# Modulation vectors of a diffusion layer: raw weight tiles of 64 rows by two column halves

## The chip, the cores and the metric

The kernel runs on one core of a Trainium2 chip. The metric is the device time of one execution in microseconds (us). The kernel before was run three times: 2631.08 us in the median, 2630.84 to 2632.65. A core has five engines, each with its own in-order list of instructions: TensorE (PE in the profile; its weight loads are listed apart as PEld), VectorE (DVE), ScalarE (ACT), GpSimd (POOL) and SyncE (SP). SP computes nothing; it issues nearly all transfers. The transfers themselves are moved by 16 DMA engines, which all queues share.

## The reference

One layer over 1024 latent tokens and 256 context tokens of width 1024, all in float32. A first FFN (width 2816), then a mixer (a short gated convolution and grouped-query attention, merged), then a second FFN. Each is normalised and modulated by vectors that come from two conditioning vectors, one for the latent and one for the context tokens. The change concerns only how these vectors are computed:

```python
mod_lat = (silu(c)     @ w_mod + b_mod)      # w_mod: 1024 x 9216
mod_ctx = (silu(c_ctx) @ w_mod + b_mod)
ml, mc = split(mod_lat, 9), split(mod_ctx, 9)   # nine vectors of 1024 each
# first FFN: shift ml[0], scale ml[1], gate ml[2]; mixer: 3, 4, 5; second FFN: 6, 7, 8
# context tokens use mc[0] to mc[4] here
```

So `w_mod` (37.7 MB) is read once, for one or two rows on the left: a matrix-vector product per conditioning vector (a "stream").

## The kernel before

All matrix products are split into a high and a low part (float32r) and made of three matmuls each, with 512 moving columns. The FFNs and the mixer's input products use a seven-product scheme (`Winograd`), whose left operands are weight tiles of 128 columns, fetched to one of three `raw` buffers, split by ScalarE (high part) and VectorE (low part) or first summed by GpSimd.

The modulations are numbered 0 to 8, and each is done in two halves of 512 columns. Modulations 0 and 1 for the latent stream are computed at the very start by other functions (`first_mod`, `second_mod`), for both streams only the first half of modulation 1. The rest are "later modulations", and `later_mod` (L272) computes them. For each half it takes eight raw tiles of 128 rows by 512 columns of `w_mod`, 256 KB each (L285). VectorE multiplies each tile, row by row, by a column of `silu_c`, and adds it to an accumulator `macc`, a tile of 128 x 512 for each stream (L289 and L291). The accumulator then has to be summed over its 128 partitions. It is split into two parts (L298), TensorE multiplies both by a single column of ones (L304, L305), ScalarE copies the resulting row of 512 out of PSUM in an order that suits the next step (L307), one transfer turns the row into four columns (L311), and VectorE adds the bias (L313).

`later_mod` is a generator. A call of `run(steps, n)` in the main loops advances it by n steps, and so its work lies between the products of the main computation. One half is 19 steps: eight with a load and its multiplications, four of waiting (`WAIT`), six more after the split, one at the end. In the first products, run by column tile j, `STEPS` (L42) gives 7 or 6 steps a tile for j up to 12, 11 from 14 on, and in between two for each of 14 context products. Modulation 1 (second half, context only), modulation 0 (context only), the context's first normalisation and modulations 2 to 4 (both streams) come in that order (`all_later_mods`, L1160). Modulation 5 is advanced 8 steps at a time from the mixer's input products (L1361), 6 and 7 8 steps at a time from the attention heads' products (L1442), and 8 by 3 steps a tile in the second FFN (L1828). For 6 and 7 the raw tiles come from a larger pool: four tiles of 512 KB for each half, fetched together (`by_four`, L277 and `fetch_mod`, L316).

Elsewhere the raw tiles and the accumulators come from a pool of eleven tiles of 128 x 512 that they share with the partial results of the main products (`ttile`, L116). The order of the instructions on each engine comes from the framework's scheduler, which plans with its own costs, except where an instruction is pinned (`pinned=True`, `strict`). All recorded operations show line L90, that of a helper, so that the views are read by the names of the tiles.

Of the kernel before, what the change touches and what calls it, by code (L numbers as in the profile page):

```python
# [9 lines left out]
F32 = mybir.dt.float32  # L10
F32R = mybir.dt.float32r
I32 = mybir.dt.int32
AF = mybir.ActivationFunctionType
ALU = mybir.AluOpType
# [4 lines left out]
P = 128  # L19
D = 1024  # L20
KD = D // P
# [22 lines left out]
WAIT = 4  # L44
# [7 lines left out]
def tile_dit_layer(  # L52
# [44 lines left out]
    act, dve, pool, pe, sp = (Engine(e) for e in (nc.scalar, nc.vector, nc.gpsimd, nc.tensor, nc.sync))  # L97

    const = ctx.enter_context(tc.tile_pool(name="const", bufs=1))
# [9 lines left out]
    def uniq(s):  # L109
        n_tiles[0] += 1  # L110
        return f"{s}_{n_tiles[0]}"

    def atile(name, shape=(P, SLOT), dt=F32):
        return apool.tile(list(shape), dt, tag="A", name=uniq(name))

    def ttile(name, n=512, dt=F32):  # L116
        t = tpool.tile([P, 512], dt, tag="t", name=uniq(name))
        return t[:, :n]

    def small(name, n, dt=F32):  # L120
        return spool.tile([P, n], dt, tag=f"s{n}_{name}", name=uniq(name))
# [4 lines left out]
    def ps_t(n=512):  # L126
        return psum.tile([P, 512], F32, tag="t", name=uniq("pt"), bufs=2)[:, :n]
# [4 lines left out]
    def matmul(out, w, x, start, stop, pinned=False, on=False):  # L132

        inst = pe.matmul(out, w, x, start=start, stop=stop, skip_group_check=on)
        if pinned:
            tc.keep_in_program_order(inst)
# [7 lines left out]
    def load(out, in_, pinned=False):  # L144
        inst = sp.dma_start(out=out, in_=in_)
        if pinned:
            tc.keep_in_program_order(inst)
# [6 lines left out]
    ones_r = const.tile([P, 1], F32R, name="ones_r")  # L154
# [4 lines left out]
    bcol = const.tile([P, 72], F32, name="bcol")  # L159
# [26 lines left out]
    def col(name, k=0):  # L186
        o = voff[name] + k
        return cols[:, o : o + 1]

    silu_c = const.tile([P, 16], F32, name="silu_c")  # L190
    act.activation(out=silu_c[:], in_=cols[:, :16], func=AF.Silu)

    modl = const.tile([P, 72], F32, name="modl")
    modc = const.tile([P, 40], F32, name="modc")


    def split(src, hi, lo, lo_eng=None, hi_eng=None):

        if hi_eng is dve:
            dve.tensor_copy(out=hi, in_=src)  # L200
        else:
            act.copy(out=hi, in_=src)
        (lo_eng or dve).tensor_sub(out=lo, in0=src, in1=hi.bitcast(F32))
# [65 lines left out]
            transpose(pr[:, j * P : (j + 1) * P], y[:, j : j + 1].to_broadcast([P, P]), pinned=True)  # L269
        return pr  # L270

    def later_mod(m, halves=(0, 1), streams=None, by_four=False):  # L272

        if streams is None:
            streams = (0, 1) if m < 5 else (0,)
        for half in halves:
            raws = fetch_mod(m, half, False) if by_four else None  # L277
            accs = [ttile(f"macc{v}") for v in streams]
            o = m * D + half * 512
            for k in range(KD):  # L280
                if by_four:
                    raw = raws[k // 2][:, k % 2]
                else:
                    raw = ttile("rawm")
                    load(out=raw, in_=w_mod[0, k * P : (k + 1) * P, o : o + 512])  # L285
                for acc, v in zip(accs, streams):
                    s = silu_c[:, v * 8 + k : v * 8 + k + 1]
                    if k == 0:
                        dve.tensor_scalar(out=acc, in0=raw, scalar1=s, scalar2=None, op0=ALU.mult)  # L289
                    else:  # L290
                        dve.scalar_tensor_tensor(out=acc, in0=raw, scalar=s, in1=acc, op0=ALU.mult, op1=ALU.add)  # L291
                yield
            for _ in range(WAIT):
                yield
            parts = []
            for acc in accs:
                ah, al = ttile("acch", dt=F32R), ttile("accl", dt=F32R)
                split(acc, ah, al)  # L298
                parts.append((ah, al))
            for _ in range(6):  # L300
                yield
            for (ah, al), v in zip(parts, streams):
                mod, pm = (modl, modc)[v], ps_t()
                matmul(pm[:1], ones_r[:], ah, start=True, stop=False, pinned=True)  # L304
                matmul(pm[:1], ones_r[:], al, start=False, stop=True, pinned=True)  # L305
                row = ttile("mrow")
                act.copy(  # L307
                    out=row[:1].rearrange("o (p j) -> o j p", j=4), in_=pm[:1].rearrange("o (j p) -> o j p", j=4)
                )
                mcol = small("mcol", 4)  # L310
                sp.dma_start(out=mcol[:], in_=row[:1])  # L311
                c0 = m * 8 + half * 4
                dve.tensor_add(out=mod[:, c0 : c0 + 4], in0=mcol[:], in1=bcol[:, c0 : c0 + 4])  # L313
            yield

    def fetch_mod(m, half, pinned=True):  # L316
        raws = []
        for kk in range(KD // 2):
            raw = atile("rawm", (P, 2, 512))
            o = m * D + half * 512  # L320
            load(raw[:], w_mod[0, kk * 256 : (kk + 1) * 256, o : o + 512].rearrange("(a p) n -> p a n", p=P), pinned)
            raws.append(raw)
        return raws
# [65 lines left out]
    def part_gain(t, m, gname, s, a, b):  # L389
        mod, c0, o = (modl if s == "l" else modc), (m + 1) * 8, voff[gname]  # L390
        dve.tensor_scalar(
            out=t[:, a:b], in0=mod[:, c0 + a : c0 + b], scalar1=1.0, scalar2=math.sqrt(D), op0=ALU.add, op1=ALU.mult
        )
        dve.tensor_mul(out=t[:, a:b], in0=t[:, a:b], in1=cols[:, o + a : o + b])
# [47 lines left out]
    def modulated_norm(xs, hh, hl, ch, gain, mod, m):  # L442

        s, o, n = ch
        acc = sum_squares(xs, ch)
        for _ in range(3):
            yield
        y = rstd_cols([acc], n, D)
        for _ in range(WAIT if m else WAIT + 3):
            yield  # L450
        pr = bcast(y, n)
        for k in range(KD):
            if k:
                yield
            t = ttile("nt", n)
            dve.tensor_mul(out=t, in0=xs(k, ch), in1=pr)
            dve.tensor_scalar(
                out=t, in0=t, scalar1=gain[s][:, k : k + 1], scalar2=mod[s][:, m * 8 + k : m * 8 + k + 1],
                op0=ALU.mult, op1=ALU.add,
            )  # L460
            split(t, hh(k, ch), hl(k, ch))
        yield
# [638 lines left out]
    for k in range(4):  # L1101
        if k % 2:
            half1.shifted(h0[k][:, 0], k, xh[k])
        else:
            dve.tensor_scalar(
                out=h0[k][:, 0], in0=xh[k], scalar1=gain1["l"][:, k : k + 1], scalar2=modl[:, k : k + 1],
                op0=ALU.mult, op1=ALU.add,
            )
        half1.keep(1, k, h0[k][:, 0])
    start = half1.start_by_half()  # L1110
# [46 lines left out]
    hc = Context("h1ch", F32R), Context("h1cl", F32R)  # L1157
    normc = modulated_norm(xc, *hc, CC, gain1, mods, 0)

    def all_later_mods():  # L1160
        yield from later_mod(1, (1,), (1,))
        yield from later_mod(0, (0, 1), (1,))
        part_gain(gain1["c"], 0, "g1", "c", 0, 8)
        for _ in normc:
            yield
        for m in range(2, 5):
            yield from later_mod(m)

    steps = all_later_mods()
    mix_steps, late_steps, last_steps = later_mod(5), (step for m in (6, 7) for step in later_mod(m, by_four=True)), later_mod(8)  # L1170

# [64 lines left out]
    for j in range(NH):  # L1236
        half1.side = side(j) if j >= SIDE_FROM else None
        u, c = half1.next_first()
        v, b = half1.second(u)
# [115 lines left out]
    for i in range(KD):  # L1355
# [6 lines left out]
        for ch, bg, gc in mixed():  # L1362
            gate(gcd, i, ch, gc)
            o = ch[1]
            y = ttile("y")
            dve.tensor_scalar(out=y, in0=u[:, o : o + 512], scalar1=col("w1", i), scalar2=None, op0=ALU.mult)
            for j in (0, 2):
                a, b = max(o, 1 - j), min(o + 512, L + 1 - j)
                ya = y[:, a - o : b - o]
                dve.scalar_tensor_tensor(  # L1370
                    out=ya, in0=u[:, a + j - 1 : b + j - 1], scalar=col(f"w{j}", i), in1=ya, op0=ALU.mult, op1=ALU.add
# [383 lines left out]
    for ch in (C0, C1):  # L1755
        o = ch[1]
        for d in range(KD):
# [7 lines left out]
                out=xs(d, ch), in0=ps, scalar=modl[:, 40 + d : 41 + d], in1=xs(d, ch), op0=ALU.mult, op1=ALU.add  # L1765
# [12 lines left out]
        out=gf[:], in0=cols[:, voff["gf"] : voff["gf"] + 8], scalar1=math.sqrt(D), scalar2=None, op0=ALU.mult  # L1778
# [47 lines left out]
    for j in range(NH):  # L1826
# [3 lines left out]
        v, b = fast.second(u)  # L1830
# [81 lines left out]
```

## Time and profile before

| | before |
|---|---|
| median of three runs | 2631.08 us |
| span of the profiled execution (the page gives no other time of it) | 2631.1 us |
| TensorE busy | 2609.9 us, 99% |
| VectorE busy | 1997.4 us, 76% |
| ScalarE busy | 1183.5 us, 45% |
| GpSimd busy | 545.8 us, 21% |
| moved by DMA | 384.69 MB, 146 GB/s |

The page lists, for each engine, how long it was busy and how many instructions it ran; then the span in 40 slices; then the DMA queues with packets, megabytes and the share of the sixteen engines' time; then the chain of work that ended last; then groups of equal instructions by `out<-in`, with count, total busy time and mean duration in ns, and behind the bar the idle time before them and what ended it. The waits view lists who waited for whom, in us, times, and the longest. `rawm` is a raw tile of `w_mod`, `macc` an accumulator, `acch` and `accl` its two parts, `mrow` the summed row, `mcol` the columns, `modl` and `modc` the finished vectors of the two streams.

### The profile page before, as it was taken

To read this page: it belongs to the slowest core of one execution; us is meant where nothing else is said; L and a number is where in the kernel's file an instruction comes from. 1 tells how busy PE (TensorE), PEld (TensorE's weight loads), DVE (VectorE), ACT (ScalarE), POOL (GpSimd) and SP (SyncE) were. 2 spreads that over 40 slices of the span, in tenths; PEclk is the share of its full clock that TensorE was granted. 3 is DMA by queue.
4 is the path that set the end of the run, shared out by engine and by line. 5 is a ranking of instruction groups with operands and counts; after the bars stand their busy time and mean duration, and the time that the engine had idled before them with its cause. 6 is when DMAs were issued, how large, how long until landed. Compare 5 with 4: busy or idle time off the path is not lost.

```text
span 2631.1 us, 35379 instructions
## 1 busy us (share of the span) xinstructions
PE 2609.9 (99%) x12665; PEld 2176.1 (83%) x12665; DVE 1997.4 (76%) x3360; ACT 1183.5 (45%) x2343; POOL 545.8 (21%) x425
## 2 busy tenths in 40 slices
PE   8999999999999999999999999999999999999998
PEld 5888899888888888888888888888888888888888
DVE  5888976877897879977788576676457886667996
ACT  6533454333454642333355566574237333334553
POOL 0133201221010034333022112132000442321100
PEclk9999999999999999999999999999999999999999
DMA  8665465345973365542522322113425653227831
GB/s 324 205 210 182 149 215 173 106 131 185 327 184 117 124 205 160 163 134 89 200 77 85 86 87 65 33 37 118 158 85 176 201 167 96 90 80 286 191 84 65
DMA packets 372905, 384.69 MB, mean 146 GB/s; under 512 B 19686, under 2 KB 256376, under 8 KB 372728
## 3 DMA queue, kind: packets, MB, share of 16 engines
q1 hardware_dynamic: 363288, 363.52, 42.1%
q0 software_dynamic: 9440, 18.91, 4.3%
q8 instruction: 99, 1.62, 0.2%
q14 instruction: 78, 0.64, 0.1%
HBM read 310.45 MB, written 71.86 MB: 145 GB/s over the span
## 4 chain that ended last, share of the span: by engine, by line
PE 94%; DVE 3%; DMA 1%; ACT 1%; issue 1%; SPq 0%; DVEq 0%; ACTq 0%
PE ps L90 81%; PE pt L90 8%; PE po L90 6%; DMA rawm<-in_w_mod_dram 1%; DVE xb L90 0%; DVE wl L90 0%; DVE macc L90 0%; DVE m L90 0%; DVE y L90 0%; DVE pts L90 0%; DMA xtok<-in_x_dram 0%; DVE x L90 0%; DVE r L90 0%; SPq L90 0%; DVE rs_t L90 0%
## 5 line engine op out<-in xcount | busy, mean ns | idle before, releaser
L90 PE MATMUL ps<-r,wl 128*128 128x512 f32 x5196 | 1198.3, 390 | 3.6 <-ACT r L90 1.3
L90 PEld LDWEIGHTS ps<-r,wl 128*128 128x128 f32 x5196 | 972.4, 188 | 207.7 <-ACT r L90 1.6
L90 ACT CAST wl<-sum 128x512 fp32r<-128x512 f32 x218 | 134.1, 622 | 294.4 <-PE ps L90 227.1
L90 ACT CAST wl<-raw 128x512 fp32r<-128x512 f32 x287 | 178.2, 622 | 193.1 <-PE ps L90 147.9
L90 DVE TENSOR_TENSOR wl<-raw,wl 128x512 fp32r<-128x512 f32 x287 | 210.2, 736 | 61.0 <-ACT wl L90 59.3
L90 DVE TENSOR_TENSOR wl<-sum,wl 128x512 fp32r<-128x512 f32 x218 | 196.9, 904 | 33.5 <-ACT wl L90 32.3
L90 POOL TENSOR_TENSOR sum<-raw 128x512 f32<-128x512 f32 x55 | 76.4, 1389 | 680.6 <-DMA raw<-in_ffn_w_in_dram 345.3
L90 DVE SCALAR_TENSOR_TENSOR macc<-rawm,silu_c,macc 128x512 f32<-128x512 f32 x178 | 145.4, 835 | 17.1 <-DMA rawm<-in_w_mod_dram 16.6
L90 DVE TENSOR_TENSOR u<-u,ps 128x512 f32<-128x512 f32 x186 | 126.5, 680 | 32.2 <-PE ps L90 32.1
L90 ACT CAST rh<-hid 128x512 fp32r<-128x512 f32 x132 | 82.2, 623 | 139.4 <-PE ps L90 112.3
L90 POOL TENSOR_TENSOR sum<-raw,sum 128x512 f32<-128x512 f32 x55 | 76.7, 1395 | 287.0 <-DVE wl L90 284.0
L90 DVE TENSOR_TENSOR pts<-pt,pts 128x512 fp32r<-128x512 f32 x160 | 107.3, 686 | 36.2 <-ACT pts L90 34.6
L90 DVE TENSOR_REDUCE m<-ps 128x1 f32<-128x256 f32 (+1 forms) x192 | 111.0, 597 | 29.4 <-PE ps L90 28.5
L90 ACT CAST pts<-pt 128x512 fp32r<-128x512 f32 x160 | 92.2, 597 | 85.5 <-PE pt L90 84.4
L90 PE MATMUL ps<-rh,wl 128*128 128x512 f32 x360 | 122.8, 390 | 0.0
L90 PE MATMUL ps<-wh,r 128*128 128x512 f32 x384 | 120.7, 392 | 0.0
L90 DVE TENSOR_TENSOR rl<-hid,rh 128x512 fp32r<-128x512 f32 x132 | 91.0, 693 | 29.9 <-ACT rh L90 19.4
L90 ACT CAST wh<-raw 128x512 fp32r<-128x512 f32 (+1 forms) x85 | 68.2, 803 | 95.5 <-PE ps L90 74.9
L90 PE MATMUL ps<-kl,qs 128*128 128x512 f32 x384 | 104.0, 394 | 0.1
L90 PE MATMUL ps<-rh,wh 128*128 128x512 f32 x300 | 102.8, 389 | 0.0
L90 PE MATMUL ps<-y,wc 128*128 128x512 f32 x384 | 95.3, 391 | 0.2 <-DVE g L90 0.2
L90 POOL TENSOR_TENSOR sum<-sum,raw 128x512 f32<-128x512 f32 x55 | 87.8, 1597 | 5.7 <-PE ps L90 3.9
(325 smaller groups left out, 5102.3 us busy)
## 6 DMA issues: line engine op xcount, KB each, us to landing
raw<-in_ffn_w_in_dram SPq DMA_DIRECT2D x131, 512.0 KB
raw<-in_ffn_w_out_dram SPq DMA_DIRECT2D x72, 512.0 KB
raw<-in_w_in_dram SPq DMA_DIRECT2D x64, 512.0 KB
rawm<-in_w_mod_dram SPq DMA_DIRECT2D x104, 256.0 KB
hid<-hd SPq DMA_DIRECT2D x40, 512.0 KB
ucd<-uc SPq DMA_DIRECT2D x33, 512.0 KB
rawm<-in_w_mod_dram SPq DMA_DIRECT2D x32, 512.0 KB
ws<-in_ffn_w_out_dram POOLq DMA_DIRECT2D x26, 512.0 KB, 6.4
```

The source lines that it names most:

```text
L90: inst = getattr(self.engine, name)(*args, **kw)
```

## The change

`later_mod` now takes a modulation's two halves together, in tiles of 64 rows by all 1024 columns. The left half of the columns goes to partitions 0 to 63 of a raw tile of 128 x 512, the right half to partitions 64 to 127, by one transfer of 256 KB whose source is a view of three dimensions (half, row, column). There are 16 such tiles for a modulation instead of twice eight, so as many transfers and as many multiplications. The column by which a tile is multiplied has to hold the same 64 numbers twice, so `spread_silu` builds `silu_r` from `silu_c` by four small transfers between SBUF tiles, issued before the later modulations begin. The accumulator holds the left half's sums in its upper 64 partitions and the right half's in its lower 64; two one-hot columns (`halves_r`) instead of one of ones sum each half apart, in one pair of matmuls with a result of two rows. Two transfers instead of one turn these rows into columns.

A modulation is now 16 + 4 + 6 + 1 = 27 steps instead of 38. The calls that advance it are unchanged. For modulations 6 and 7 the four larger tiles are each filled by two transfers of 256 KB. The one half that remains alone (modulation 1, second half) keeps the old form as `later_half`.

```diff
+    one_hot = const.tile([P, 2], F32, name="one_hot")
+    pool.memset(one_hot[:], 0.0)
+    for h in range(2):
+        pool.memset(one_hot[h * 64 : (h + 1) * 64, h : h + 1], 1.0)
+    halves_r = const.tile([P, 2], F32R, name="halves_r")
+    act.copy(out=halves_r[:], in_=one_hot[:])
+    silu_r = const.tile([P, 32], F32, name="silu_r")
+
+    def spread_silu():
+        by = silu_r[:].rearrange("p (a s) -> p a s", s=2)
+        for h in range(2):
+            for i in range(2):
+                sp.dma_start(out=by[h * 64 : (h + 1) * 64, :, i], in_=silu_c[i * 64 : (i + 1) * 64, :])
...
-    def later_mod(m, halves=(0, 1), streams=None, by_four=False):
+    def later_mod(m, streams=None, by_four=False):
...
-        for half in halves:
-            raws = fetch_mod(m, half, False) if by_four else None
-            accs = [ttile(f"macc{v}") for v in streams]
-            o = m * D + half * 512
-            for k in range(KD):
-                if by_four:
-                    raw = raws[k // 2][:, k % 2]
+        def rows(t):
+            return w_mod[0, t * 64 : (t + 1) * 64, m * D : (m + 1) * D].rearrange("r (h n) -> h r n", h=2)
+
+        accs = [ttile(f"macc{v}") for v in streams]
+        for t in range(16):
+            if by_four and t % 8 == 0:
+                raws = []
+                for i in range(4):
+                    raw = atile("rawm", (P, 2, 512))
+                    for a in range(2):
+                        load(raw[:, a], rows(t + 2 * i + a))
+                    raws.append(raw)
+            if by_four:
+                raw = raws[t % 8 // 2][:, t % 2]
+            else:
+                raw = ttile("rawm")
+                load(raw, rows(t))
+            for acc, v in zip(accs, streams):
+                s = silu_r[:, v * 16 + t : v * 16 + t + 1]
...
+        yield from mod_sums(accs, streams, m * 8, halves_r, 2)
...
+    def mod_sums(accs, streams, c0, sums, n):
...
+        for (ah, al), v in zip(parts, streams):
+            mod, pm = (modl, modc)[v], ps_t()
+            matmul(pm[:n], sums[:], ah, start=True, stop=False, pinned=True)
+            matmul(pm[:n], sums[:], al, start=False, stop=True, pinned=True)
...
+            mcol = small("mcol", 8)
+            for h in range(n):
+                sp.dma_start(out=mcol[:, h * 4 : (h + 1) * 4], in_=row[h : h + 1])
+            dve.tensor_add(out=mod[:, c0 : c0 + 4 * n], in0=mcol[:, : 4 * n], in1=bcol[:, c0 : c0 + 4 * n])
...
+    spread_silu()
+
     def all_later_mods():
-        yield from later_mod(1, (1,), (1,))
-        yield from later_mod(0, (0, 1), (1,))
+        yield from later_half(1, 1, (1,))
+        yield from later_mod(0, (1,))
```

More of the change, by code (lines that the diff above doesn't have):

```diff
@@ L270, in bcast @@
         return pr
-    def later_mod(m, halves=(0, 1), streams=None, by_four=False):
+    def later_mod(m, streams=None, by_four=False):
         if streams is None:
             streams = (0, 1) if m < 5 else (0,)
-        for half in halves:
-            raws = fetch_mod(m, half, False) if by_four else None
-            accs = [ttile(f"macc{v}") for v in streams]
-            o = m * D + half * 512
-            for k in range(KD):
-                if by_four:
-                    raw = raws[k // 2][:, k % 2]
-                else:
[L284 to L313, printed above, removed]
-            yield
@@ new lines, in rows @@
+        def rows(t):
[16 more added lines that the diff above has]
+                s = silu_r[:, v * 16 + t : v * 16 + t + 1]
+                if t == 0:
+                    dve.tensor_scalar(out=acc, in0=raw, scalar1=s, scalar2=None, op0=ALU.mult)
+                else:
+                    dve.scalar_tensor_tensor(out=acc, in0=raw, scalar=s, in1=acc, op0=ALU.mult, op1=ALU.add)
+            yield
@@ new lines, in later_mod, with later_half @@
+        yield from mod_sums(accs, streams, m * 8, halves_r, 2)
+    def later_half(m, half, streams):
+        accs = [ttile(f"macc{v}") for v in streams]
+        o = m * D + half * 512
+        for k in range(KD):
+            raw = ttile("rawm")
+            load(out=raw, in_=w_mod[0, k * P : (k + 1) * P, o : o + 512])
+            for acc, v in zip(accs, streams):
+                s = silu_c[:, v * 8 + k : v * 8 + k + 1]
+                if k == 0:
+                    dve.tensor_scalar(out=acc, in0=raw, scalar1=s, scalar2=None, op0=ALU.mult)
+                else:
+                    dve.scalar_tensor_tensor(out=acc, in0=raw, scalar=s, in1=acc, op0=ALU.mult, op1=ALU.add)
+            yield
+        yield from mod_sums(accs, streams, m * 8 + half * 4, ones_r, 1)
@@ new lines, in mod_sums @@
+    def mod_sums(accs, streams, c0, sums, n):
+        for _ in range(WAIT):
+            yield
+        parts = []
+        for acc in accs:
+            ah, al = ttile("acch", dt=F32R), ttile("accl", dt=F32R)
+            split(acc, ah, al)
+            parts.append((ah, al))
+        for _ in range(6):
+            yield
+        for (ah, al), v in zip(parts, streams):
+            mod, pm = (modl, modc)[v], ps_t()
+            matmul(pm[:n], sums[:], ah, start=True, stop=False, pinned=True)
+            matmul(pm[:n], sums[:], al, start=False, stop=True, pinned=True)
+            row = ttile("mrow")
+            act.copy(
+                out=row[:n].rearrange("o (p j) -> o j p", j=4), in_=pm[:n].rearrange("o (j p) -> o j p", j=4)
+            )
+            mcol = small("mcol", 8)
+            for h in range(n):
+                sp.dma_start(out=mcol[:, h * 4 : (h + 1) * 4], in_=row[h : h + 1])
+            dve.tensor_add(out=mod[:, c0 : c0 + 4 * n], in0=mcol[:, : 4 * n], in1=bcol[:, c0 : c0 + 4 * n])
+        yield
```

## The prediction

> **What bounds the kernel now.** I read the page first: the span, the engines' busy time, the queue that carries the transfers, the chain that ended last.
>
> ```profile
> span 2631.1 us, 35379 instructions
> PE 2609.9 (99%) x12665; PEld 2176.1 (83%) x12665; DVE 1997.4 (76%) x3360; ACT 1183.5 (45%) x2343; POOL 545.8 (21%) x425
> ...
> q1 hardware_dynamic: 363288, 363.52, 42.1%
> ...
> PE 94%; DVE 3%; DMA 1%; ACT 1%; issue 1%; SPq 0%; DVEq 0%; ACTq 0%
> ```
>
> TensorE is busy 99% of the span and is 94% of the chain. Whatever leaves TensorE shortens the time; whatever leaves VectorE or ScalarE does not; and anything that makes TensorE wait for its weights lengthens the time directly. The sixteen DMA engines are 42.1% busy with the queue that SyncE (SP) feeds: slack on average, as long as all sixteen share it.
>
> Next the waits, SyncE's own queue first, then VectorE's.
>
> ```profile
> SPq L90 <- DVE wl L90: 480.9, 142, 44.7
> ...
> SPq L90 <- DVE macc L90: 18.0, 13, 6.8
> ...
> SPq L90 <- DMA rawm<-in_w_mod_dram: 9.0, 14, 1.8
> ```
>
> ```profile
> DVE macc L90 <- DMA rawm<-in_w_mod_dram: 25.0, 21, 4.0
> ```
>
> SyncE waits longest (480.9 us) until the splitting of a weight tile frees its buffer: weights are fetched as early as a buffer is free, so a stock of fetched weights normally lies ready. The modulation's accumulation waits for its own transfers only 25.0 us in all, so these transfers are prompt today.
>
> **The change, part by part.** The groups that the change touches:
>
> ```profile
> L90 PE MATMUL ps<-r,wl 128*128 128x512 f32 x5196 | 1198.3, 390 | 3.6 <-ACT r L90 1.3 <-DVE r L90 0.8 <-ACT uc L90 0.7
> ...
> L90 DVE SCALAR_TENSOR_TENSOR macc<-rawm,silu_c,macc 128x512 f32<-128x512 f32 x178 | 145.4, 835 | 17.1 <-DMA rawm<-in_w_mod_dram 16.6
> ...
> L90 ACT COPY mrow<-pt 1x512 f32<-1x512 f32 x23 | 24.2, 1079 | 16.9 <-PE pt L90 16.9
> ...
> L90 DVE TENSOR_TENSOR accl<-macc,acch 128x512 fp32r<-128x512 f32 x26 | 17.7, 686 | 2.2 <-ACT acch L90 2.0
> ...
> L90 ACT CAST acch<-macc 128x512 fp32r<-128x512 f32 x26 | 16.2, 622 | 34.2 <-DVE macc L90 32.7 <-DMA hid<-hd 1.5
> ...
> L90 DVE TENSOR_SCALAR macc<-rawm,silu_c 128x512 f32<-128x512 f32 x26 | 12.8, 510 | 8.4 <-DMA rawm<-in_w_mod_dram 8.4
> ...
> L90 PE MATMUL pt<-acch,ones_r 128*1 128x512 f32 x23 | 9.1, 396 | 0.0
> L90 PE MATMUL pt<-accl,ones_r 128*1 128x512 f32 x23 | 9.1, 396 | 0.0
> ```
>
> *Sums over partitions (TensorE).* There are 23 of them, one per half and stream: 1 for the second half of modulation 1, 2 for modulation 0, 12 for 2 to 4, 8 for 5 to 8. After, one serves both halves: 1 + 1 + 6 + 4 = 12. Eleven pairs go, 22 matmuls. One lasts 396 ns, but matmuls overlap: the largest group takes 1198.3 us for 5196, 0.231 us each, and that is what a matmul costs on the path. Gain: 22 x 0.231 = 5.1 us. Two stationary columns instead of one change nothing I can price: the moving 512 columns are the same.
>
> *ScalarE and VectorE.* Eleven casts (622 ns), eleven copies (1079 ns) and eleven subtractions (686 ns) go; the accumulating operations stay 16 per modulation and stream, with eleven first ones (510 ns) turned into later ones (835 ns), +3.6 us of VectorE. Net -18.7 us of ScalarE and -3.9 us of VectorE, at 45% and 76% busy: nothing on the path; TensorE's 99% covers it, and if that cover went, the gain would be at most these amounts.
>
> *Set-up.* The memsets and the copy for the one-hot columns are a handful of instructions in the first microseconds: 0. Four transfers copy 4-byte elements, 1024 each, and sit on SP's queue ahead of the later modulations' loads.
>
> ```profile
> rinvd<-rinv POOLq DMA_DIRECT2D x16, 2.0 KB, 8.6
> ...
> mcol<-mrow SPq DMA_DIRECT2D x23, 2.0 KB
> ```
>
> The nearest row is the 2 KB of 4-byte elements that lands in 8.6 us. Four such in a row, each twice as many elements, are 69 us if nothing overlaps, and nearly 0 if the elements spread over the engines behind the stock of weights. I take 0, since the first user comes 20 steps later; the upper end belongs to the range. The column transfers stay 23 (two for each of 11, one for the half), and their sums cost the same.
>
> *The accumulators* hold one of eleven shared tiles per stream for 20 steps instead of 12. The 18.0 us that SyncE waits for them bound that from above; I take 0.
>
> *The transfers.* This part decides. Until now a raw tile is 128 rows of 2 KB, with 128 as the outermost count on both sides. Now the source is 2 halves of 64 rows: its outermost count is 2, because no single step leads from the 64th row of one half to the first row of the other. How such a transfer is shared among the sixteen engines no row of before shows. If it is cut by its outermost dimension, only two pieces can be made, and two engines carry it; if by rows, sixteen carry it. The price comes from the early stretch in which little but such rows is moved:
>
> ```profile
> DMA packets 1594, 4.02 MB, mean 365 GB/s; under 512 B 118, under 2 KB 140, under 8 KB 1594
> ...
> q1 hardware_dynamic: 1594, 4.02, 97.1%
> ...
> rawm<-in_w_mod_dram SPq DMA_DIRECT2D x8, 512.0 KB
> ```
>
> That window is 3 to 14 us: 0.971 x 16 x 11 = 171 us of engine time for 4.02 MB, 42.5 us per MB. A raw tile of 0.262 MB takes 11.1 us of engine time: 0.70 us on sixteen engines, 5.6 us on two. I take two: the cut needs a dimension that both ends have, and the destination's 128 partitions and the source's 2 x 64 rows agree in nothing outermost but 2. The Trainium skill, "DMA: Bandwidth & Descriptors" (the section on why a DMA increments its semaphore by 16, and its rules for kernel authors), says as much: the engine count is the largest up to 16 that divides both sides' slowest dimension, and an outermost dimension of size c confines the whole transfer to c engines. No run here shows it yet; by it the sum is the one that follows, and by a cut into rows the sum would be only the 5.1 us gained.
>
> Eight modulations (0 and 2 to 8) have 16 such loads each. The weights' loads are queued behind them on the same SP queue, and a sixteenth of every weight tile still passes the two busy engines. On VectorE, the multiplication by a raw tile waits, with the splits of weights and of attention operands queued behind it, and TensorE behind those. A stretch of loads therefore takes what the two engines need: loads x 5.6 us plus their ordinary share. How fast the loads come is set by the steps. The column transfers mark 19 steps per half (8 loads, then 4 + 6 + 1 empty):
>
> ```profile
> 177.85 0.56 SPq L90 DMA_DIRECT2D mcol<-mrow  x1
> 262.30 0.48 SPq L90 DMA_DIRECT2D mcol<-mrow  x1
> 408.27 0.48 SPq L90 DMA_DIRECT2D mcol<-mrow  x1
> 636.75 0.48 SPq L90 DMA_DIRECT2D mcol<-mrow  x1
> 1131.86 0.47 SPq L90 DMA_DIRECT2D mcol<-mrow  x1
> 1227.57 0.48 SPq L90 DMA_DIRECT2D mcol<-mrow  x1
> 1291.01 0.47 SPq L90 DMA_DIRECT2D mcol<-mrow  x1
> 1338.53 0.48 SPq L90 DMA_DIRECT2D mcol<-mrow  x1
> 2148.27 0.48 SPq L90 DMA_DIRECT2D mcol<-mrow  x1
> 2252.11 0.48 SPq L90 DMA_DIRECT2D mcol<-mrow  x1
> ```
>
> First column: the start. Two halves, 38 steps, from 177.9 to 262.3: 2.2 us a step in the first products. Four halves from 408.3 to 636.8: 3.0. One from 1131.9 to 1227.6 (mixer): 5.0. Three from 1291.0 to 1338.5 (heads): 0.83. One from 2148.3 to 2252.1 (second FFN): 5.5. The same stretches by windows; the last two columns are the DMA share and GB/s:
>
> ```profile
> 177.80:262.30 84.50, 84.50 (x374) 69.46 (x373) 74.47 (x102) 28.48 (x49) 34.25 (x24) 1.00 0.63 197
> 262.30:322.00 59.70, 59.70 (x277) 49.83 (x276) 55.94 (x103) 25.42 (x51) 17.41 (x12) 1.00 0.44 141
> ...
> 408.30:636.70 228.40, 228.31 (x1240) 196.49 (x1239) 177.32 (x267) 88.27 (x155) 51.02 (x32) 1.00 0.39 125
> ...
> 1131.90:1227.60 95.70, 95.70 (x424) 79.02 (x423) 71.34 (x111) 31.70 (x53) 30.50 (x20) 1.00 0.35 113
> ...
> 1291.00:1338.50 47.50, 47.50 (x217) 38.63 (x216) 42.00 (x111) 17.92 (x54) 8.34 (x16) 1.00 0.40 133
> ...
> 2148.30:2252.10 103.80, 103.80 (x459) 85.77 (x458) 73.25 (x101) 33.69 (x56) 32.31 (x22) 1.00 0.37 116
> ```
>
> From each share I take off the raw tiles' own part (0.70 us each). A modulation is now 16 loads and 11 empty steps, so the loads come as densely as before but in runs of 16. Excess = loads x 5.6 + share x time - time:
> - modulation 0: 16 loads in 36 us, share 0.50: 90 + 18 - 36 = 72
> - modulation 2: the shorter steps of 0 let it begin 11 steps earlier, among the first products: 11 loads in 24 us, 0.44: 62 + 11 - 24 = 49; its other 5 in 15 us, 0.29: 28 + 4 - 15 = 17
> - modulations 3 and 4: 16 loads in 48 us, 0.29: 90 + 14 - 48 = 56 each
> - modulation 5: 16 in 81 us, 0.29: 90 + 23 - 81 = 32
> - modulations 6 and 7: 32 in 54 steps, 45 us, 0.16: 179 + 7 - 45 = 141 (16 more issues on SP than now, nothing beside that)
> - modulation 8: 16 in 87 us, 0.32: 90 + 28 - 87 = 31
>
> Together 454 us. Against it stands the stock. Two of the three weight buffers lie ready; a pair feeds five products of twelve matmuls, 60 x 0.231 = 13.9 us, and a little is already split: 15 us for each of eight stretches, 120 us. Net +334, less 5.1: 2631.1 + 329 = 2960 us. The span (2631.1) equals the median of the runs (2631.08), so nothing needs adding around it.
>
> Ends: with no stock +454; with the whole queue's price (42.1% x 16 x 2631.1 us / 363.52 MB = 48.8 us per MB, 6.4 us a tile) another 0.8 x 128 = 102; with the set-up's 69 us beyond a stock of 15 another 54: 3236. With a stock of 30 us everywhere (the split tiles too) the eight terms shrink to 227; with the loads also spread into the empty steps, 5 and 8 vanish and 3 and 4 halve, about 130; with the heads' term halved too, because only VectorE and not the weights waits there, about 75: 2701.
>
> **The rivals.**
> *Shared by rows.* Sixteen engines carry the new transfer, 0.70 us each, as now. For it: bytes, row length and destination partitions are the old ones. Against it: the count of 2 in front. Then only the 22 matmuls count: 2631.1 - 5.1 = 2626.0, not slower. It decides if more than about ten engines carry a tile: up to 1.1 us, loads at 2.2 us a step leave room. The Trainium skill, in the same page's rules for kernel authors, advises one 128-partition transfer over two for the halves, since both use the same engines; that speaks for this side if the source's count does not matter, and the sum by it would be these 2626.0.
> *Two engines, but hidden.* On average they have room: 0.421 x 2631.1 + 128 x (5.6 - 0.7) = 1735 us of 2631. If loads came no closer than every 10 us (5.6 over the free share of 0.56), nothing would stall: also 2626.0. Against it: steps of 0.83 to 5.5 us.
> *VectorE becomes the bound*, its operations held in order behind raw tiles: in the sum already, as the heads' 141; if that delay ran in full in every stretch, that is the end without stock, 3080. It has no chance of its own.
>
> **How the numbers follow.** Two engines with stalls 0.85, by rows 0.11, two engines hidden 0.04. The likeliest gives 2960. Between its ends, 2700 to 3230, lies some 0.95 of its chance, 0.81 of the whole, so the range need not reach to the rivals; it is slower throughout. A measurement of this kernel can tell about 0.2%, 5.3 us, from no change. The rivals' -5.1 us sits at that edge: of their 0.15, 0.06 faster, 0.06 within, and 0.03 slower through the set-up transfers or the accumulators. Slower in all 0.88.
>
> **What would show it.** Right: as many bytes moved, VectorE's wait of macc for rawm in hundreds of us instead of 25.0; TensorE's busy share falling below 93% with gaps in the stretches above, the heads' the largest; GB/s in those stretches falling well under the values above; 12 pairs of partition sums. Wrong: rawm waits of tens of us and TensorE still at 99%, which means that sixteen engines shared the tiles; or waits only in the heads, which means that the stock covered the rest.

## The result and the profile after

| | before | after |
|---|---|---|
| median of four runs | 2631.42 us | 3084.92 us (3080.86 to 3087.14) |
| span of the profiled execution | 2631.1 us | 3082.0 us |

The ratio is 1.1718 (95%: 1.1702 to 1.1735): 17% slower, 453.5 us. (Of the six runs of the version with rows outermost, tried below, one took 3732.22 us at a granted clock of 0.653 and is left out of its ratio; its 2640.1 us is the same with or without that run.) The page of the kernel after, its heads, engines, slices of TensorE and its clock, and SP's queue:

```profile
span 3082.0 us, 35318 instructions
PE 2711.3 (88%) x12643; PEld 2232.4 (72%) x12643; DVE 1973.8 (64%) x3338; ACT 1160.7 (38%) x2322; POOL 533.6 (17%) x428
...
PE   8976869586999999869943799999999978999999
...
PEclk9988989797999999989976899999999989999999
...
q1 hardware_dynamic: 365912, 363.53, 36.3%
```

The same 363.5 MB are moved in more time, so the mean share of the DMA engines falls (42.1% to 36.3%) while VectorE waits 442.1 us for raw tiles: the mean over sixteen engines hides what two of them do. TensorE's idle time is span less busy: 21.2 us before, 370.7 us after, so 349.5 of the 450.9 us of longer span. The other 101.4 us are a longer busy time, although 22 matmuls fewer ran: the second row of digits shows the clock below 9 tenths only in slices where TensorE has gaps. (The chain of waits can't be read here: the page follows it over 15% of the span and then loses it.)

The waits and groups of after that answer to those shown of before, VectorE's, SyncE's, TensorE's and the two groups that were priced:

```profile
DVE macc L90 <- DMA rawm<-in_w_mod_dram: 442.1, 120, 7.2
...
PE ps L90 <- DVE wl L90: 162.9, 47, 17.8
```

```profile
SPq L90 <- DVE wl L90: 597.2, 153, 45.8
...
SPq L90 <- DVE macc L90: 34.9, 11, 5.4
```

```profile
L90 PE MATMUL ps<-r,wl 128*128 128x512 f32 x5196 | 1266.7, 403 | 160.6 <-DVE wl L90 112.0
...
L90 DVE SCALAR_TENSOR_TENSOR macc<-rawm,silu_r,macc 128x512 f32<-128x512 f32 x165 | 122.1, 756 | 413.9 <-DMA rawm<-in_w_mod_dram 413.9
```

TensorE's wait for the low part of the weight tiles, 162.9 us, was this before:

```profile
PE ps L90 <- DVE wl L90: 0.7, 2, 0.4
```

VectorE's wait for raw tiles went from 25.0 to 442.1 us, in 120 pieces of at most 7.2 us. That number lies so near the loss that it invites a conclusion; the third experiment shows why it would be the wrong one.

How a raw tile comes is best seen in the heads, where from 1549 to 1662 us nothing else is loaded. First the transfers of that window, then VectorE's timeline:

```profile
GB/s 67 51 51 49 49 50 50 49 58 51 49 49 50 50 49 49 51 49 49 50 50 49 49 51 49 49 50 50 49 49 51 49 46 50 49 50 49 50 50 49
...
q1 hardware_dynamic: 2808, 5.65, 13.2%
```

```profile
1565.54 0.75 DVE L90 SCALAR_TENSOR_TENSOR macc<-rawm,silu_r,macc 128x512 f32<-128x512 f32 x1 [4.51 <-DMA rawm<-in_w_mod_dram]
...
1581.37 0.75 DVE L90 SCALAR_TENSOR_TENSOR macc<-rawm,silu_r,macc 128x512 f32<-128x512 f32 x1 [4.45 <-DMA rawm<-in_w_mod_dram]
1586.64 0.75 DVE L90 SCALAR_TENSOR_TENSOR macc<-rawm,silu_r,macc 128x512 f32<-128x512 f32 x1 [4.45 <-DMA rawm<-in_w_mod_dram]
1591.91 0.75 DVE L90 SCALAR_TENSOR_TENSOR macc<-rawm,silu_r,macc 128x512 f32<-128x512 f32 x1 [4.45 <-DMA rawm<-in_w_mod_dram]
```

13.2% of sixteen engines is 2.1 engines, and 0.132 x 16 x 113 us for 5.65 MB is 42.2 us of engine time per MB, the 42.5 of the prediction. A tile comes every 5.27 us (1581.37, 1586.64, 1591.91). Two engines carry it. The rule of the Trainium skill that the prediction weighed ("DMA: Bandwidth & Descriptors", the section on why a DMA increments its semaphore by 16) agrees with this row.

Where the time went by stretch shows in when the same instructions are issued, first before, then after, in SP's timeline (start, duration): the 13th store `hd<-c` (of the first column tile behind the context products), the first `gcd<-b` of the mixer, the last `yd<-y`, the first `zd<-g` behind the heads, the last `hd<-c` of the second FFN.

```profile
461.14 0.33 SPq L90 DMA_DIRECT2D hd<-c  x1
971.20 0.57 SPq L90 DMA_DIRECT2D gcd<-b  x1
1249.45 0.33 SPq L90 DMA_DIRECT2D yd<-y  x1
1429.91 0.32 SPq L90 DMA_DIRECT2D zd<-g  x1
2399.91 0.37 SPq L90 DMA_DIRECT2D hd<-c  x1
```

```profile
632.61 0.33 SPq L90 DMA_DIRECT2D hd<-c  x1
1197.58 0.57 SPq L90 DMA_DIRECT2D gcd<-b  x1
1528.24 0.33 SPq L90 DMA_DIRECT2D yd<-y  x1
1829.54 0.32 SPq L90 DMA_DIRECT2D zd<-g  x1
2850.68 0.69 SPq L90 DMA_DIRECT2D hd<-c  x1
```

The delay stands at 171.5, 226.4, 278.8, 399.6 and 450.8 us. It grows where raw tiles are loaded; between the heads and the second FFN's first store, where none are, it moves from 399.6 to 400.3.

### The profile page after: what moved, and what is told of

Its sections match the earlier page's. It is cut to its first block, busy times and chain, and to the rows that moved or that the text cites. A ratio compares the mean times of both kernels' runs of the same rounds, so it can differ in the third digit from the quotient of the medians.

```text
span 3082.0 us, 35318 instructions
## 1 busy us (share of the span) xinstructions
PE 2711.3 (88%) x12643; PEld 2232.4 (72%) x12643; DVE 1973.8 (64%) x3338; ACT 1160.7 (38%) x2322; POOL 533.6 (17%) x428
## 3 DMA queue, kind: packets, MB, share of 16 engines
q1 hardware_dynamic: 365912, 363.53, 36.3%
## 5 line engine op out<-in xcount | busy, mean ns | idle before, releaser
L90 PE MATMUL ps<-r,wl 128*128 128x512 f32 x5196 | 1266.7, 403 | 160.6 <-DVE wl L90 112.0
L90 PEld LDWEIGHTS ps<-r,wl 128*128 128x128 f32 x5196 | 1003.8, 195 | 400.6 <-DVE wl L90 133.6
L90 DVE SCALAR_TENSOR_TENSOR macc<-rawm,silu_r,macc 128x512 f32<-128x512 f32 x165 | 122.1, 756 | 413.9 <-DMA rawm<-in_w_mod_dram 413.9
L90 PE MATMUL ps<-h1ch,wl 128*128 128x256 f32 x448 | 95.6, 311 | 37.1 <-DVE wl L90 33.0
L90 ACT ACTIVATE c<-c 128x512 f32<-128x512 f32 x46 | 29.1, 632 | 254.4 <-DMA c<-ucd 163.8
L90 PEld LDWEIGHTS ps<-h1ch,wl 128*128 128x128 f32 x448 | 80.7, 217 | 41.9 <-DVE wl L90 35.1
```

The costliest lines, as they stand in the source:

```text
L90: inst = getattr(self.engine, name)(*args, **kw)
```

## The experiments

The theory was the prediction's: the count of 2 in front puts the tile on two engines, and what waits behind them makes the loss. Rivals: it is not the transfer but the new layout (steps, sums); it is VectorE's in-order wait; it is the density of the loads. Each version is compared with runs of the kernel before on the same chip; on the three chips used, their median was 2631.5, 2631.5 and 2632.7 us. A time without an interval is that of one run. In the code cuts, "..." stands for lines left out.

### Two transfers for a tile

Against the kernel after; each half of a tile by a transfer of 64 rows of its own.

```diff
-        def rows(t):
-            return w_mod[0, t * 64 : (t + 1) * 64, m * D : (m + 1) * D].rearrange("r (h n) -> h r n", h=2)
+        def load_rows(raw, t):
+            for h in range(2):
+                o = m * D + h * 512
+                load(raw[h * 64 : (h + 1) * 64], w_mod[0, t * 64 : (t + 1) * 64, o : o + 512])
...
```

> The changed kernel, but each raw tile is filled by two transfers of 64 rows x 512 columns, one per half, so that the outermost count is 64 on both sides. Two-engines theory: the whole loss goes; VectorE's wait of macc for rawm falls from 442 us to tens, and only the 5.1 us of TensorE are left as a gain: 2626 us (2620 to 2640). Rival theory, that the loss comes from the rest of the change (runs of 16 loads, 27 steps instead of 38, accumulators held longer, the four set-up transfers): still above 3000 us.

Measured: 2660.31 us, ratio to before 1.0108 (1.0095 to 1.0121). VectorE's wait:

```profile
DVE macc L90 <- DMA rawm<-in_w_mod_dram: 31.1, 23, 6.0
```

425 of the 453 us are gone with the same tiles, sums and steps. The rival layout is out as the main cause. The expectation (2620 to 2640) missed: 29 us stay, of which 19 arise before the 12th store `hd<-c` (317.8 to 336.9 us).

### One transfer with the rows outermost

Against the kernel after; row r of half h now goes to partition 2r + h. The one-hot columns go by parity (VectorE makes them now), `silu_r` is filled with a step of 2 partitions.

```diff
-            return w_mod[...].rearrange("r (h n) -> h r n", h=2)
+            return w_mod[...].rearrange("r (h n) -> r h n", h=2)
...
```

> The changed kernel, still with one transfer per raw tile, but partition 2r+h holds row r of half h, so that the source's outermost count is 64 (rows) and the halves come second; one-hot columns and silu_r follow by parity of the partition. Two-engines theory: only the outermost count matters, so 2626 us (2620 to 2640), about as the kernel with two transfers and 128 fewer transfers on SP. Rival theory, that one transfer from two places 2 KB apart is slow in any order (or that the rest of the change costs): about 3085 us.

Measured: 2640.1 us, ratio 1.0032 (1.0019 to 1.0045). VectorE's wait:

```profile
DVE macc L90 <- DMA rawm<-in_w_mod_dram: 16.3, 12, 3.1
```

One transfer, the same bytes, only another order of the two counts, and of the rows over the same 128 partitions: 445 us apart. It is still 8.6 us above the kernel before, at the upper end of what was expected.

### VectorE waits for no raw tile

Against the kernel after; all transfers stay, but VectorE multiplies a resident identity tile instead of the raw tile (so modulations 0 and 2 to 8 leave their weights out).

```diff
-                    dve.scalar_tensor_tensor(out=acc, in0=raw, scalar=s, in1=acc, op0=ALU.mult, op1=ALU.add)
+                    dve.scalar_tensor_tensor(out=acc, in0=still, scalar=s, in1=acc, op0=ALU.mult, op1=ALU.add)
...
```

> The changed kernel with all its transfers, two engines each, but VectorE multiplies the identity tile instead of the raw tile, so that no engine waits for a raw tile; modulations 0 and 2 to 8 are left without their weights. VectorE theory (the multiplications wait in order and hold the splits of the weights behind them, so that the stock of fetched weights cannot help): most of the 454 us goes, 2631 to 2720 us. Weights theory (the weight transfers themselves are late because a sixteenth of each stands behind raw tiles on the two engines, as the prediction's sum has it): most of it stays, 2900 to 3085 us.

Measured: 3060.36 us, and the same places lose (heads 119 us instead of 121). The 442.1 us of waiting for raw tiles is gone and the loss is not: that wait is not needed for it. What TensorE waits for in the heads (1540 to 1830 us), in the kernel after and in this one:

```profile
PE pt L90 <- ACT acch L90: 60.7, 2, 59.4
PE pt L90 <- DVE xb L90: 35.7, 1, 35.7
PE ps L90 <- DVE wl L90: 17.8, 1, 17.8
```

```profile
PE pt L90 <- DVE xb L90: 99.6, 1, 99.6
PE ps L90 <- ACT wh L90: 16.2, 1, 16.2
```

In the kernel after, one wait is 59.4 us: the pinned matmul of a modulation's sum stands on TensorE until the slow tiles have come. Here no sum waits for tiles, and TensorE waits 99.6 us once for `xb`, an operand of the attention, instead. VectorE could not make `xb`, because ahead of it stood the last step of a modulation, and that step's columns were late. VectorE's and SP's timelines of this run:

```profile
1659.67 0.17 DVE L90 TENSOR_TENSOR modl<-mcol,bcol 128x8 f32<-128x8 f32 x1 [104.02 <-DMA mcol<-mrow]
```

```profile
1521.80 123.55 SPq L90 DMA_DIRECT2D rawm<-in_w_mod_dram  x25
1645.45 5.72 SPq L90 DMA_DIRECT2D mcol<-mrow  x2
```

SP needed 123.55 us for the issue of 25 raw tiles, 4.9 us each, and the transfer of the columns, queued behind, was issued only then. So whoever does not wait for the raw tiles waits for what stands behind them on SP. In the kernel after the same step stands ahead of the `xb` for which TensorE waited 35.7 us:

```profile
1682.63 0.17 DVE L90 TENSOR_TENSOR modl<-mcol,bcol 128x8 f32<-128x8 f32 x1 [26.00 <-DMA mcol<-mrow]
```

VectorE's list in order is therefore still part of how the delay reaches TensorE; only the raw tiles need not be what it waits for.

### The kernel before with a count in front

Against the kernel before, with its halves, sums and steps: only the source of the later modulations' loads gets an outermost count of 2, 4 or 16; for modulations 6 and 7 a tile of 512 KB is filled by two such loads.

```diff
-                    load(out=raw, in_=w_mod[0, k * P : (k + 1) * P, o : o + 512])
+                    load(out=raw, in_=w_mod[0, k * P : (k + 1) * P, o : o + 512].rearrange("(r q) n -> q r n", q=2))
...
```

> The kernel before, with one change: the later modulations' loads take their 128 rows in another order, even rows to partitions 0 to 63 and odd rows to 64 to 127, by a source view whose outermost count is 2 (and modulations 6 and 7 fetch each 512 KB tile by two such transfers). Rows and silu then do not belong together, so these modulations are other numbers. Two-engines theory: the transfer alone brings the loss, in runs of 8 instead of 16 loads: 3000 to 3085 us, a raw tile every 5.3 us where they stall. Rival theory (the rest of the change costs): 2631 us.

> As the kernel before with even and odd rows apart, but four groups of rows (row 4r+q to partition 32q+r), an outermost count of 4; the modulations are again other numbers. Two-engines theory: four engines, 2.8 us a tile; by the prediction's sum without a stock of weights, stretch by stretch, about 95 us: 2726 us (2680 to 2770). Rival theory, that any source that is not 128 rows in a row is slow by a fixed amount per transfer: about 3078 us, as with the count of 2.

> The same with sixteen groups of rows (row 16r+q to partition 8q+r), an outermost count of 16; the modulations are again other numbers. Two-engines theory: all sixteen engines again, so 2631 us (2626 to 2640), although the order of the rows is as scattered and modulations 6 and 7 still fetch by twice as many transfers. Rival theory (the scattered order or the extra transfers cost): well above 2650 us.

Measured: 3078.2 us with a count of 2, 2770.82 with 4, 2637.9 with 16; spans 3076.4, 2769.1 and 2636.1, so +445, +138 and +5 us. The count alone brings nearly the whole loss (450.9 by the spans), in the old runs of eight loads too, and the scattered rows with their extra loads bring some 5 us (the count of 16 is the control). VectorE's timeline with a count of 4, in the heads:

```profile
1375.36 0.75 DVE L90 SCALAR_TENSOR_TENSOR macc<-rawm,silu_c,macc 128x512 f32<-128x512 f32 x1 [1.83 <-DMA rawm<-in_w_mod_dram]
1377.92 0.75 DVE L90 SCALAR_TENSOR_TENSOR macc<-rawm,silu_c,macc 128x512 f32<-128x512 f32 x1 [1.40 <-DMA rawm<-in_w_mod_dram]
1380.48 0.75 DVE L90 SCALAR_TENSOR_TENSOR macc<-rawm,silu_c,macc 128x512 f32<-128x512 f32 x1 [1.14 <-DMA rawm<-in_w_mod_dram]
```

A tile every 2.56 us, half of 5.27: four engines. The loss is not halved but falls to a third, and most where the steps are slow: behind the heads from 47 to 9 us, up to the 13th store `hd<-c` from 146 to 55. The prediction's formula, even without its stock, was too mild here: 95 us against 138.

### Fewer steps a call in the heads

Against the kernel after.

```diff
-            run(late_steps, 8)
+            run(late_steps, 2)
```

> The changed kernel as it is, but the attention heads' products advance modulations 6 and 7 by 2 steps a call instead of 8, so that their 32 slow tiles lie over all 26 calls instead of the first 7. Theory of the density (a stretch takes what the two engines need, the rest is hidden): the heads' loss falls from 121 us to some 40, so 3005 us (2985 to 3030). Rival theory (each slow tile costs the same wherever it lies, 121/32 = 3.8 us): 3085 us.

Measured: 3067.64 us; the heads lose 103 us instead of 121. Missed, between the two expectations. SP's timeline (from 1530 to 1640 us) shows that the edit did not do what it was for:

```profile
1544.35 74.04 SPq L90 DMA_DIRECT2D rawm<-in_w_mod_dram  x16
```

The eight loads of a group are one step, and they still go out back to back, 4.6 us each on SP.

### Single tiles in the heads, two steps a call

Against the kernel after; modulations 6 and 7 take single tiles from the shared pool, so that each load is a step.

```diff
-(step for m in (6, 7) for step in later_mod(m, by_four=True))
+(step for m in (6, 7) for step in later_mod(m))
...
-            run(late_steps, 8)
+            run(late_steps, 2)
```

> The changed kernel, but modulations 6 and 7 take their raw tiles one by one from the shared pool of eleven, as the other modulations do, and the heads' products advance them by 2 steps a call; so the 32 slow loads are really issued over all 26 calls and not in groups of eight. Theory of the density: the two engines need 179 us plus a share of 0.2 x 165 us for a stretch of 165 us, an excess of 47 us in place of the heads' 121: 3011 us (2985 to 3035). Rival theory (each slow tile costs 3.8 us wherever it lies): 3085 us.

Measured: 3062.03 us, heads 97 us. Missed again. SP's timeline, the same window:

```profile
1544.41 75.43 SPq L90 DMA_DIRECT2D rawm<-in_w_mod_dram  x16
```

All sixteen loads of modulation 6 are issued in one run although the steps that use them lie apart; those of modulation 7 do come in pieces, from 1659 to 1752 us. So for modulation 6 the steps did not set when loads are issued; perhaps the scheduler puts a load as early as a buffer is free, which was not tested by itself. What spread loads would cost in the heads is not shown by either run.

### Rows outermost, with the old density

Two edits on the version with the rows outermost, for its 8.6 us. First only the first products' steps:

```diff
-STEPS = (0, 7, 7, 7, 6, 6, 6, 6, 6, 6, 6, 6, 6, 0, 11)
+STEPS = (0, 6, 6, 6, 6, 5, 5, 5, 5, 5, 5, 5, 5, 0, 11)
```

> The kernel with rows outermost (one fast transfer per tile), and the first products advance the modulations by 6 and 5 steps a tile instead of 7 and 6 (64 instead of 75 steps until the context products, which is what modulations 1 and 0 and the first normalisation now need). Theory of the denser steps: what is left of the loss arises where modulation 2 now begins 11 steps earlier, in a stretch where VectorE is already about 89% busy; without them 2626 us (2620 to 2634), below the kernel before. Rival theory (one-hot sums, set-up transfers or longer-lived accumulators cost it): 2640 us again.

Measured: 2635.81 us, ratio 1.0016 (1.0007 to 1.0025), between the two expectations. A cause shows in the windows from 165 to 340 us: in the kernel before and in the one with rows outermost, first VectorE's and ScalarE's work on `macc`, then the busy times of all five engines (TensorE, its weight loads, VectorE, ScalarE, GpSimd):

```profile
165.00:340.00 175.00, 20.71 (x25) 1.25 (x2) 1.00 0.59 184
165.00:340.00 175.00, 175.00 (x834) 146.68 (x833) 155.03 (x240) 68.10 (x123) 58.51 (x40) 1.00 0.59 184
```

```profile
165.00:340.00 175.00, 32.95 (x41) 0.62 (x1) 1.00 0.59 185
165.00:340.00 175.00, 171.12 (x798) 140.22 (x796) 154.90 (x248) 60.57 (x111) 57.89 (x40) 1.00 0.59 185
```

Shorter modulations pull 16 operations more, 12 us, into a stretch in which VectorE was already 155.03 of 175 us busy. Its total does not rise (154.90): as much of its other work moves out of the window, and TensorE loses 3.9 us there. With fewer steps the delay at the 12th store `hd<-c` falls from 13.7 to 1.4 us, but only about half of the 8.6 us at the end is gone. Then every pace was set to the old density:

```diff
-STEPS = (0, 7, 7, 7, 6, 6, 6, 6, 6, 6, 6, 6, 6, 0, 11)
-BATCH = 2
+STEPS = (0, 6, 6, 6, 6, 5, 5, 5, 5, 5, 5, 5, 5, 0, 9)
+BATCH = 1
...
-            run(mix_steps, 8)
+            run(mix_steps, 6)
...
-            run(late_steps, 8)
+            run(late_steps, 6)
...
-            run(last_steps, 3)
+            run(last_steps, 2)
```

> The kernel with rows outermost (one fast transfer per tile), with every place that advances the modulations slowed to the old density: 6 and 5 steps a tile in the first products, 1 instead of 2 per context product, 9 instead of 11 behind them, 6 instead of 8 in the mixer and the heads, 2 instead of 3 in the second FFN. Theory of the denser steps: the small stalls that are left go, and the 5.1 us of TensorE show: 2627 us (2622 to 2632). Rival theory (the new order of instructions costs a few us whatever the density): 2636 us, as with the first products alone.

Measured: 2628.68 us against 2632.70, ratio 0.9985 (0.9976 to 0.9994). This version beats both kernels, by 4.0 us over the one before: little, but with an interval that leaves out 1. The first products' steps are worth 4.3 us of the way from 8.6 above to 4.0 below, the other paces the rest.

## Why the prediction was right, and where it was wrong

The sign, the cause and the range were right; the forecast of 2960 us was 125 us too low.

- *Two engines carry a tile*: shown three ways (2.1 engines' time in use; +445, +138 and +5 us for counts of 2, 4 and 16; all but 8.6 us gone with the rows outermost). 5.6 us a tile was 5.27.
- *Shared by rows* and *two engines, but hidden* fell with it. The rule for one transfer instead of two that the prediction cited from the Trainium skill (same page, rules for kernel authors) does not hold where the one transfer has a 2 in front: 3084.92 us against 2660.31 for two. It does where the rows are in front: 2640.1.
- *22 matmuls, 5.1 us*: 11 pairs with the one-hot columns and one with ones ran behind the set-up, as foreseen. Only once the loads are spread as before is the kernel faster, by 4.0 us; that this is the matmuls' 5.1 fits by size and was not shown apart.
- *ScalarE and VectorE off the path*: ScalarE's busy time fell by 22.8 us (18.7 foreseen), VectorE's by 23.6 (3.9 foreseen; 10.8 us are the same 50 operations `u<-u,v`, 810 ns each instead of 1025, and the later accumulations were shorter too, 756 ns instead of 835), and neither bought time. But "nothing on the path" was too simple: the shorter modulations put more VectorE work into the first products, and thinning their steps there took off 4.3 of the 8.6 us.
- *Set-up transfers and accumulators at 0*: SP waited 34.9 us for accumulators instead of 18.0, but 17.4 us with the rows outermost, so it follows the slow tiles. The best version contains both and loses nothing.
- *The excess by stretch*, without the stock, beside the measured growth of the delay and the growth of TensorE's idle time in it (window less busy time, between the issues shown above):

| stretch | foreseen | measured | of it TensorE idle |
|---|---|---|---|
| to the 13th store `hd<-c`: 0, 2, about three quarters of 3 | 180 | 171.5 | 118.4 |
| to the mixer: rest of 3, and 4 | 70 | 54.9 | 41.9 |
| mixer: 5 | 32 | 52.4 | 40.7 |
| heads: 6 and 7 | 141 | 120.8 | 114.2 |
| behind the heads: 8 | 31 | 51.2 | 33.9 |
| sum | 454 | 450.8 | 349.1 |

- *The stock, 15 us for each of eight stretches, 120 us*: by the sum this is the term that was too large. The end without stock, 454 less 5.1, is 449 us, and 450.9 were measured. A stock is there: modulation 0's first tile is issued at 178.47 us and TensorE's first gap of more than a microsecond behind it ends at 196.02 us. Two things suggest why a stock of weights is of little help. In the heads, 95 us of TensorE's waiting were for a sum and for `xb`. And SP itself was held while it issued, so that transfers other than weights came late too, for which the sum had no price.
- *How far that match of 449 and 450.9 is luck*: in part it is. The stretches are off by 8 to 20 us both ways, and with a count of 4 the same formula without stock gave 95 us for 138. A second account fits the total as well: TensorE's idle time grew by 349.5 us, near the 334 that the prediction had with its stock, and the other 101.4 us are longer busy time, most of it at a lower clock, a term that the prediction left out. The runs do not decide between the two.
- *The range's lower end, 2701 us*, does not come out of its own terms: 227 less the 3 us of modulations 5 and 8 and half of the 52 of 3 and 4 is 198, not about 130, and with half of the heads' 111 off, the end is some 2768. The measured time lies far above either.
- *VectorE as the bound, 3080 us without stock*: its number is nearly the measured one, its reason is not shown. Without any wait of VectorE for raw tiles the kernel still took 3060.36 us, though there VectorE stood 104.02 us in order behind late columns.
- *What would show it*: the wait of `macc` (442.1), TensorE below 93% (88%) and 12 pairs came. GB/s in the modulation 0 stretch fell from 197 to 95. The gaps are largest in the heads, as single waits (59.4 us), though the loss up to the 13th store `hd<-c` is larger in sum.

Open: why two transfers for a tile cost 20 us more than one with the rows outermost (they are 128 more issues on SP; not tried by themselves), how the lateness divides between SP's held issue and the packets queued on the two busy engines, and what a lower density of loads in the heads would be worth.

## What to carry to other kernels

Look at the outermost count on both sides of a transfer before its bytes: the same 256 KB came every 5.27 us with a 2 in front, with 64 rows there VectorE waited 16.3 us in all, and swapping two counts of a view was worth 445 us. A wait nearly as long as the loss need not be its cause: take the wait away and leave the transfer, and see whether the time comes back. And a step that gets shorter makes its neighbours denser; a change that removes steps has to set their pace anew before its gain can show.

## What the runs showed of the hardware

SP is held while it issues. A raw tile's issue took 0.4 us in the median before; in the kernel after, each takes about 5 us once some of the slow tiles are outstanding, and so can what comes next on SP, here a store of 256 KB, an FFN weight and a read of `ucd` in modulation 0's stretch:

```profile
202.00 5.81 SPq L90 DMA_DIRECT2D hd<-c  x1
207.85 5.76 SPq L90 DMA_DIRECT2D rawm<-in_w_mod_dram  x2
214.04 4.68 SPq L90 DMA_DIRECT2D raw<-in_ffn_w_in_dram  x1
218.82 5.41 SPq L90 DMA_DIRECT2D u<-ucd  x1
```

So a slow transfer delays the issue of others behind it: the weight tile's alone took 4.68 us. And TensorE's clock falls where it has gaps: the windows of that stretch and of the heads, kernel after (window, length, busy times of the five engines, clock, DMA share, GB/s), against a clock of 1.00 in every window of before that the prediction shows.

```profile
177.80:262.30 84.50, 49.41 (x174) 36.91 (x172) 30.43 (x48) 10.55 (x18) 10.92 (x8) 0.82 0.29 95
...
1549.00:1662.00 113.00, 39.55 (x171) 31.77 (x169) 26.31 (x65) 11.45 (x43) 1.96 (x4) 0.70 0.13 50
```

TensorE's busy time grew by 101.4 us in all; the granted clock over its busy stretches, summed from the trace, accounts for about 92 of them. What part of this lengthened the kernel, and what part only filled gaps that were there anyway, the runs do not separate.
